# A two-layer hybrid decoder trunk on one core: another planning of its order, an earlier first weight block, and another start

## The chip, the cores and the metric

The kernel runs on one core of a Trainium2 chip. The metric is the device time of one execution in microseconds: the median of 3 runs before is 1589.41 us (1588.22 to 1592.01).

## What is computed

Two layers over 512 positions of width 1024, all in float32. Cut to what matters:

```python
for i in range(2):
    h = rmsnorm(x, mix_pre_g[i]);  z = h @ w_in[i]              # 1024 -> 3206 columns, split over three mixers
    # A: chunked causal spatial gating on u, v;  B: chunkwise retention on q, k, v, g (6 heads, rotary)
    # C: forgetting attention on q, k, v, f (6 heads, softmax over s <= t)
    x = x + rmsnorm(concat(A, B, C) @ w_o[i], mix_post_g[i])
    h = rmsnorm(x, ffn_pre_g[i])
    g = causal_dwconv3(h @ w_gate[i]);  f = (gelu(g) * (h @ w_up[i])) @ w_down[i]      # 1024 -> 4096 -> 1024
    x = x + rmsnorm(f, ffn_post_g[i])
    gate = sigmoid(rmsnorm(x, ple_pre_g[i]) @ w_ple_gate[i])
    x = x + rmsnorm((p[i] @ w_ple_proj[i]) * gate, ple_post_g[i])
```

## The kernel before

The program is written as a list of operations, and a planner (class Plan) decides their order on each engine. It keeps every operation with its reads, writes and an estimated cost, plays them through a model of the engines, and gives each engine the earliest recorded operation among those that are ready; then all operations are issued in that order. An operation may take a buffer ahead of the oldest unfinished operation only within a number of operations that belongs to its stage (AHEAD: mix for the mixers, wo and wo2 for the two halves of the output projection, emb for the p projection, gu0 and gu for the gate/up blocks, dn, end, pg, pg2), and only if the buffers that the recorded order needs up to there are not more than there are. There are 24 large buffers of 8 KB a partition (18 of set X, 6 of set W; wg, wsa and wsb must lie in W, other fp32r tiles in X, float32 tiles in either), 12 work tiles (wk) and 8 PSUM banks. All instructions are issued on one line (L444), so the profile is read by tile names.

Precise products are made of three fp32r matmuls: each operand is split into a rounded high part (a cast on ACT) and the rest (a subtraction on DVE), and mm3 multiplies high by high, high by low and low by high. The function split issues these two instructions. Transposes, the small attention and retention products and the cumulative sums are float32 matmuls.

The stages of a layer:

- The mixers. Plain makes hT, the transposed operand of the normed rows: for each chunk of 128 positions and each half of the columns a multiplication by the norm vector (tile gain), four transposes into hps, a split. Its scale method makes the row factors rs (square and row sum on ACT, power on POOL). The steps run in the order written in mixers: u is the gating projection (weights uv, eight blocks of k, chunk after chunk in tm_chunk_major; its PSUM tiles are called ps), F and v the other value projections, f0 to f2, r0 to r2 and g0 to g2 the projections of heads (fps, rps, gps), a0 to a2 attention, c0 to c2 the retention cores, s the spatial gating, L a silu.
- out_proj: the concatenated result cc times w_o, first all four chunks in the first half of the columns (PSUM tiles wo, the blocks of cc in O_ORDER), then the second half chunk by chunk in the order 0, 2, 1, 3. After each chunk of the second half, done normalises and stores the row and hands it to Seven, which makes the seven operands of the FFN product (tiles hb, hh, hd) by transposes, sums and splits.
- ffn: the p projection (embed, PSUM tiles eps), then 32 gate/up blocks and the down product (dn). gate_up computes a 2 x 2 block product with seven instead of eight multiplications. For each block it loads raw weights (graw, two transfers of 512 KB), splits wg and wu, forms sums and differences in place with four additions, and splits these to wsa and wsb; then seven products of 12 matmuls go to the PSUM tiles beta and ag. From block 4 on TensorE's order is fixed by a fence; before that the planner mixes.
- ple: the gate and the last residual.

At the start the program loads the rows of x chunk by chunk (512 KB each), the identity, the norm vector (a broadcast to all partitions, 512 KB) and the uv weights in four transfers of 512 KB, all from SP except the identity, which ACT issues.

## Time and profile before

| | us |
|---|---|
| median of 3 runs | 1589.41 |
| lowest, highest | 1588.22, 1592.01 |
| the profiled execution | 1587.76 |
| its span, first to last instruction | 1585.7 |
| PE busy in the span | 1559.8 (98%) |
| DVE busy | 1233.2 (78%) |
| ACT busy | 837.2 (53%) |
| DMA, mean | 125 GB/s |

Times are microseconds from the span's start. PE is TensorE's matmul row, PEld its weight loads, DVE is VectorE, ACT ScalarE, POOL GpSimd, and SPq the transfers that SyncE issues. The ends of matmuls are modelled, so the pitch of their starts says more than their durations. The clock column is the granted clock of TensorE as a share of 2.4 GHz: 1.00 or 0.50.

### The profile page before, as it was taken

The page shows a single profiled execution, that of the slowest core. Times are in us where ns is not written, and L with a number is a line of the kernel's source. Part 1 is how long each engine was busy: PE and PEld are TensorE (multiplying, and loading weights), DVE is VectorE, ACT ScalarE, POOL GpSimd, SP SyncE. Part 2 cuts the span into 40 slices and gives each one's busy share as a digit, 9 for nine tenths or more (in the row PEclk, how much of TensorE's full clock was granted, in tenths as well). Part 3 has the DMA queues.
Part 4 walks back from the last instruction along what each step waited for, and adds up shares of the span by engine and source line. Part 5 has one row for each costly group of instructions (what it writes and reads, how often), then busy time and mean ns, then how long its engine had stood idle before and what let it go on. Part 6 is the DMA issues. An engine that isn't in the chain of part 4 may idle for free.

```text
span 1585.7 us, 25202 instructions
## 1 busy us (share of the span) xinstructions
PE 1559.8 (98%) x10034; PEld 1388.1 (88%) x10034; DVE 1233.2 (78%) x2013; ACT 837.2 (53%) x1380; POOL 91.3 (6%) x157
## 2 busy tenths in 40 slices
PE   7999998999999999999999999989999999999998
PEld 6887787999999999998888777889999999999987
DVE  6556869988878888878664658699887897898785
ACT  7324637665555555554552446477655555555453
POOL 1100020000000000002220000200000000000021
PEclk9999999999999999999999999999999999999999
DMA  8113147223323422424463023362332233234433
GB/s 316 68 55 107 61 168 265 81 80 115 125 81 103 137 80 88 153 100 180 179 250 107 28 80 116 125 252 81 108 116 97 92 123 106 83 131 134 148 141 124
DMA packets 63421, 197.47 MB, mean 125 GB/s; under 512 B 7348, under 2 KB 15164, under 8 KB 63304
## 3 DMA queue, kind: packets, MB, share of 16 engines
q1 hardware_dynamic: 63160, 195.81, 35.1%
q8 instruction: 78, 1.28, 0.3%
q14 instruction: 39, 0.32, 0.1%
q10 hardware_dynamic: 144, 0.07, 0.0%
HBM read 178.52 MB, written 17.33 MB: 124 GB/s over the span
## 4 chain that ended last, share of the span: by engine, by line
PE 95%; DVE 2%; DMA 1%; ACT 1%; POOL 0%; issue 0%; SPq 0%; POOLq 0%; DVEq 0%; ACTq 0%
PE beta L444 22%; PE dn L444 22%; PE ag L444 16%; PE ps L444 15%; PE rps L444 4%; PE fps L444 4%; PE gps L444 2%; PE wo L444 2%; PE sps L444 1%; PE hps L444 1%; PE tps L444 1%; PE ops L444 1%; PE rops L444 1%; DMA graw<-in_w_gu_dram 1%; PE ips L444 0%
## 5 line engine op out<-in xcount | busy, mean ns | idle before, releaser
L444 PE MATMUL dn<-thl,act 128*128 128x512 f32 x1536 | 371.4, 391 | 0.0
L444 PEld LDWEIGHTS dn<-thl,act 128*128 128x128 f32 x1536 | 279.9, 188 | 51.9
L444 PE MATMUL ps<-thl,hT 128*128 128x512 f32 (+3 forms) x984 | 207.1, 368 | 0.1
L444 PEld LDWEIGHTS ps<-thl,hT 128*128 128x128 f32 x984 | 177.0, 189 | 23.3 <-DVE thl L444 1.2
L444 DVE TENSOR_TENSOR graw<-graw 128x512 f32<-128x512 f32 x256 | 169.2, 684 | 1.0
L444 DVE TENSOR_TENSOR thl<-traw,thl 128x1024 fp32r<-128x1024 f32 (+2 forms) x120 | 140.4, 1184 | 13.6 <-ACT thl L444 13.6
L444 ACT CAST thl<-traw 128x1024 fp32r<-128x1024 f32 (+2 forms) x120 | 120.1, 1018 | 9.0 <-DMA traw<-in_w_pg_dram 4.6
L444 PE MATMUL beta<-hh,wsa 128*128 128x256 f32 x768 | 101.4, 281 | 7.8 <-ACT gs L444 7.5
L444 PEld LDWEIGHTS beta<-hh,wsa 128*128 128x128 f32 x768 | 94.7, 192 | 8.7 <-ACT gs L444 7.9
L444 PEld LDWEIGHTS beta<-hb,wg 128*128 128x128 f32 x768 | 97.7, 189 | 4.9
L444 PEld LDWEIGHTS beta<-hh,wu 128*128 128x128 f32 x768 | 98.2, 189 | 4.2
L444 PE MATMUL beta<-hh,wu 128*128 128x256 f32 x768 | 100.4, 280 | 0.0
L444 PE MATMUL beta<-hb,wg 128*128 128x256 f32 x768 | 99.9, 278 | 0.0
L444 PE MATMUL ag<-hb,wg 128*128 128x256 f32 x768 | 98.6, 276 | 0.0
L444 PE MATMUL ag<-hd,wsa 128*128 128x256 f32 x768 | 98.5, 278 | 0.0
L444 PE MATMUL beta<-hh,wsb 128*128 128x256 f32 x768 | 98.4, 276 | 0.0
L444 DVE SCALAR_TENSOR_TENSOR cv<-gs,cw,cv 128x511 f32<-128x511 f32 (+1 forms) x128 | 95.1, 743 | 3.6 <-ACT cv L444 3.5
L444 PE MATMUL ag<-hb,wsb 128*128 128x256 f32 x768 | 97.9, 276 | 0.0
L444 ACT ACTIVATE cv<-gs,cw 128x512 f32<-128x512 f32 x64 | 52.2, 816 | 82.4 <-DVE gs L444 82.4
L444 ACT COPY gs<-beta 128x256 f32<-128x256 f32 x128 | 47.2, 371 | 88.4 <-PE beta L444 86.6
L444 DVE TENSOR_TENSOR wsb<-graw,wsb 128x1024 fp32r<-128x1024 f32 x64 | 78.0, 1219 | 19.8 <-ACT wsb L444 15.0
L444 PEld LDWEIGHTS ag<-hd,wsa 128*128 128x128 f32 x768 | 93.1, 190 | 0.0
(193 smaller groups left out, 2655.7 us busy)
## 6 DMA issues: line engine op xcount, KB each, us to landing
graw<-in_w_gu_dram SPq DMA_DIRECT2D x128, 512.0 KB, 6.2
traw<-in_w_dn_dram SPq DMA_DIRECT2D x64, 512.0 KB, 5.0
x<-x SPq DMA_DIRECT2D x40, 512.0 KB, 5.0
fraw<-in_w_fm_dram SPq DMA_DIRECT2D x30, 512.0 KB, 8.8
traw<-in_w_wo_dram SPq DMA_DIRECT2D x16, 512.0 KB, 4.2
traw<-in_w_pg_dram SPq DMA_DIRECT2D x16, 512.0 KB, 8.6
x<-in_x_dram SPq DMA_DIRECT2D x8, 512.0 KB
traw<-in_w_uv_dram SPq DMA_DIRECT2D x8, 512.0 KB, 8.1
```

Of the source, the lines that this page charges most:

```text
L444: made = o[1](*[self.map(v) for v in o[2]], **{k: self.map(v) for k, v in o[3].items()})
```

## The change

- The planner: limits ahead are other numbers, most of them larger; a buffer that all its users have left is no longer counted as occupied until its place in the recorded order (the two lines with -= 1). The costs of matmul kinds and of changes between kinds are other numbers, and its clock model stays at the upper level once reached. An operation can be put behind another (behind).
- The mixers' steps come in another order, and two blocks of cc change places in O_ORDER.
- The preparation of a gate/up block's weights is a function of its own. That of block 0 is recorded inside out_proj, after the first chunk of the second half (EARLY).
- The start: x's first chunk and the norm vector are loaded in halves of 256 KB, the former from SP, the latter from ACT; the first layer's uv weights come in eight transfers of 256 KB and are split one block of k at a time; the row factors are put behind the last of these splits in the plan. Ten bf16 matmuls of 512 columns on a tile of zeros are recorded ahead of everything.

```diff
--- before.py
+++ after.py
...
@@ -59,12 +59,12 @@
-    AHEAD = {"mix": 460, "wo": 230, "wo2": 230, "emb": 185, "gu0": 720, "gu": 460, "dn": 245, "end": 770, "pg": 450, "pg2": 120}
+    AHEAD = {"mix": 595, "wo": 404, "wo2": 214, "emb": 291, "gu0": 1206, "gu": 523, "dn": 1028, "end": 1710, "pg": 555, "pg2": 142}
     LOAD = 1290
...
     TABLES = (AF.Exp, AF.Gelu_apprx_tanh, AF.Silu, AF.Sigmoid, AF.Sin)
-    SWITCH = {"F": 110, "T": 9}
+    SWITCH = {"F": 40, "H": 310, "T": 9}
     HOP = {"PE": 197, "DVE": 128, "ACT": 131, "POOL": 80, "SP": 0}
...
@@ -189,6 +190,8 @@
                 t[2].append((i, write, r))
+        if self.behind is not None:
+            deps.add(self.behind)
         if engine == "PE":
...
@@ -220,10 +223,11 @@
             dt, rows = kw["lhsT"].dtype, kw["lhsT"].shape[0] / P
-            if dt == F32R:
+            if dt in (F32R, BF16):
                 return 0.4427 * n, 0, n * rows, n
-            half = 0.5 if kw["lhsT"].shape[0] == 64 or kw["lhsT"].shape[-1] == 64 else 1
-            return half * max(222, n * 4 / 2.4 + 4), 0, 2 * n * rows, "F"
+            if kw["lhsT"].shape[0] == 64 or kw["lhsT"].shape[-1] == 64:
+                return 0.5 * (n * 4 / 2.4 + 4), 0, 2 * n * rows, "H"
+            return max(222, n * 4 / 2.4 + 4), 0, 2 * n * rows, "F"
         if engine == "ACT":
...
@@ -356,8 +360,10 @@
                     heapq.heappush(slots[tag], now)
+                    live[tag][front:last[t] + 1] -= 1
                     if t in self.kind:
                         c, k = self.place[t]
+                        inside[c][front:last[t] + 1] -= 1
                         heapq.heappush(unused[c], (now, k))
...
@@ -402,13 +408,14 @@
                         if ops[i][6][3] != kind:
-                            busy += self.SWITCH.get(kind, 0) + (95 if ops[i][6][3] == "F" else 25 if ops[i][6][3] == 512 else 0)
+                            busy += self.SWITCH.get(kind, 0) + {"H": 95, 512: 25}.get(ops[i][6][3], 0)
                             kind = ops[i][6][3]
                     if e == "PE":
-                        if columns.get(now // self.TICK - 1, 0) < self.WARM:
+                        if not warm:
                             busy *= 2
-                        tick = (now + busy) // self.TICK
-                        columns[tick] = columns.get(tick, 0) + ops[i][6][2]
+                            tick = (now + busy) // self.TICK
+                            columns[tick] = columns.get(tick, 0) + ops[i][6][2]
+                            warm = columns.get(now // self.TICK - 1, 0) >= self.WARM
                     if self.table.get(i) not in (None, table):
...
@@ -483,7 +490,11 @@
 FM_COLS = [c + p * P for p in range(3) for c in (C_RQ, C_RK)] + [C_RG + p * P for p in range(3)] + [c + p * P for p in range(3) for c in (C_FQ, C_FK)]
-O_ORDER = (0, 1, 5, 6, 7, 2, 3, 4)
+STEPS = "u g1 F g0 f0 s v f1 a0 g2 L a1 f2 r0 r1 a2 c0 r2 c2 c1"
+O_CHUNKS = (0, 2, 1, 3)
+EARLY = {0: 0}
+O_ORDER = (0, 1, 5, 6, 7, 2, 4, 3)
+IDLE = 10
 SEVEN = ("hb11", "hb21", "hh6", "hd", "hh7", "hb22", "hh4")
...
@@ -652,11 +663,11 @@
-        def __call__(self, c, x):
+        def __call__(self, c, x, halves=range(2)):
             if self.t is None:
...
                 self.rs = small("rs", NCH)
-            for kh in range(2):
+            for kh in halves:
                 cs = slice(kh * 512, kh * 512 + 512)
...
@@ -1062,7 +1073,7 @@
         fq, rq = {}, {}
-        for step in "u F s g1 f0 g0 v a0 f1 a1 g2 r0 f2 L c0 r1 a2 r2 c1 c2".split():
+        for step in STEPS.split():
             h = int(step[1]) if len(step) > 1 else 0
...
@@ -1092,7 +1105,26 @@
-    def out_proj(l, cc, x, new, g, nxt):
+    def gate_up_weights(l, b):
+
+        stage, plan.stage = plan.stage, "gu0" if b < 4 else "gu"
+        raw = b8("graw", (2048,))
+        load(raw, a["w_gu"][l, b].rearrange("p s n -> p (s n)"))
+        u2, u1, g1, g2 = (raw[:, i * 512:i * 512 + 512] for i in range(4))
+        wg = b8("wg", (2, 1024), F32R)
+        split(wg[:, 0, :], wg[:, 1, :], raw[:, 1024:2048])
+        wu = [wk("wu", dt=F32R) for _ in range(2)]
+        split(wu[0], wu[1], u2)
+        for t, by in ((g1, u1), (u1, u2), (u2, g1), (g2, u2)):
+            V.tensor_tensor(out=t, in0=t, in1=by, op=ALU.add)
+        sa = b8("wsa", (2, 1024), F32R)
+        split(sa[:, 0, :], sa[:, 1, :], raw[:, 0:1024])
+        sb = b8("wsb", (2, 1024), F32R)
+        split(sb[:, 0, :], sb[:, 1, :], raw[:, 1024:2048])
+        plan.stage = stage
+        return wg, wu, sa, sb
+
+    def out_proj(l, cc, ready, x, new, g, nxt):
...
@@ -1114,10 +1146,15 @@
             nxt(c, x[c])
-        tm_chunk_major(cc, u, 512, done, O_ORDER, (0, 2, 1, 3))
+            if len(seen) in EARLY:
+                ready[EARLY[len(seen)]] = gate_up_weights(l, EARLY[len(seen)])
+            seen.append(c)
+
+        seen = []
+        tm_chunk_major(cc, u, 512, done, O_ORDER, O_CHUNKS)
         return emb
-    def ffn(l, hs, emb, x, new, g, nxt):
+    def ffn(l, hs, emb, ready, x, new, g, nxt):
         h = hs.t
...
@@ -1135,20 +1172,7 @@
         def gate_up(b, between):
-            raw = b8("graw", (2048,))
-            load(raw, a["w_gu"][l, b].rearrange("p s n -> p (s n)"))
-            u2, u1, g1, g2 = (raw[:, i * 512:i * 512 + 512] for i in range(4))
-            wg = b8("wg", (2, 1024), F32R)
-            split(wg[:, 0, :], wg[:, 1, :], raw[:, 1024:2048])
-            wu = [wk("wu", dt=F32R) for _ in range(2)]
-            split(wu[0], wu[1], u2)
-            for t, by in ((g1, u1), (u1, u2), (u2, g1), (g2, u2)):
-                V.tensor_tensor(out=t, in0=t, in1=by, op=ALU.add)
-            sa = b8("wsa", (2, 1024), F32R)
-            split(sa[:, 0, :], sa[:, 1, :], raw[:, 0:1024])
-            sb = b8("wsb", (2, 1024), F32R)
-            split(sb[:, 0, :], sb[:, 1, :], raw[:, 1024:2048])
-
+            wg, wu, sa, sb = gate_up_weights(l, b) if b not in ready else ready[b]
             beta, ag = bank("beta"), bank("ag")
...
@@ -1337,29 +1361,62 @@
+    idle = wk("idle", dt=BF16)
+    G.memset(idle, 0.0)
+    ps = bank("idle")
+    for i in range(IDLE):
+        T.matmul(ps, lhsT=idle[:, 0:P], rhs=idle, start=True, stop=True)
+
     x = Rows(x0)
-    x.load(0)
+    x.t[0] = b8("x", (2, D))
+    g = Gains(None, ("mix_pre_g", 0))
+    g.t = b8("gain", (2, D))
+    raws = [b8("traw", (4, 512)) for _ in range(2)]
+
+    def half(i):
+        cs = slice(i * 512, i * 512 + 512)
+        SY.dma_start(out=x[0][:, cs], in_=x0[:, 0, cs])
+        A.dma_start(out=g.t[:, 1, cs], in_=a["mix_pre_g"][0:1, cs].to_broadcast([P, 512]))
+
+    half(0)
     ident = const("ident", A)
-    g = Gains(None, ("mix_pre_g", 0))
+    SY.dma_start(out=raws[0][:, 0, :], in_=a["w_uv"][0][:, 0, :])
+    half(1)
+    for k in range(1, KB):
+        SY.dma_start(out=raws[k // 4][:, k % 4, :], in_=a["w_uv"][0][:, k, :])
     hT = Plain(g)
-    hT(0, x[0])
-    uv = tm_units(a["w_uv"][0], 512)
+    parts = []
+    for k in range(KB):
+        if k % 4 == 0:
+            hT(0, x[0], (k // 4,))
+        if k % 2 == 0:
+            parts.append(b8("thl", (2, 2, 512), F32R))
+        split(parts[-1][:, 0, k % 2, :], parts[-1][:, 1, k % 2, :], raws[k // 4][:, k % 4, :])
+
+    last = len(plan.ops) - 1
+
+    def uv(i, k, c0=0, c1=512):
+        return parts[k // 2][:, i, k % 2, c0:c1]
+
     for c in range(1, NCH):
...
         hT(c, x[c])
+    plan.behind = last
     for c in range(NCH):
         hT.scale(c, x[c])
+    plan.behind = None
     kdec = const("kdec")
...
     for l in range(DEPTH):
-        cc = mixers(l, hT, uv)
+        ready = {}
+        cc = mixers(l, hT, uv, ready)
         g = Gains(("mix_post_g", l), ("ffn_pre_g", l))
         hs = Seven(g)
-        emb = out_proj(l, cc, Rows(src), xd[3 * l], g, hs)
+        emb = out_proj(l, cc, ready, Rows(src), xd[3 * l], g, hs)
         g = Gains(("ffn_post_g", l), ("ple_pre_g", l))
         hT = Plain(g)
-        ffn(l, hs, emb, Rows(xd[3 * l]), xd[3 * l + 1], g, hT)
+        ffn(l, hs, emb, ready, Rows(xd[3 * l]), xd[3 * l + 1], g, hT)
         last = l + 1 == DEPTH
```

## Rows read from the trace of the kernel before

**Rows 1.** The head of the page: the span, and the busy time of each engine with its share and its number of instructions.

```profile
span 1585.7 us, 25202 instructions
PE 1559.8 (98%) x10034; PEld 1388.1 (88%) x10034; DVE 1233.2 (78%) x2013; ACT 837.2 (53%) x1380; POOL 91.3 (6%) x157
```

**Rows 2.** Who waited for whom, on PE, over the whole span: us in total, times, longest.

```profile
PE hps L444 <- DVE h L444: 7.9, 1, 7.9
PE beta L444 <- ACT gs L444: 7.5, 2, 3.8
PE hps L444 <- ACT wg L444: 1.8, 2, 0.9
PE cps L444 <- DVE ro L444: 1.2, 2, 0.7
```

**Rows 3.** The chain of waits in order of time: start, length, what. The first two are the first real matmuls and transposes of the second chunk, the third the rest of the gating projection.

```profile
9.95 6.26 PE ps L444 x17
16.21 0.44 PE hps L444 x4
...
21.45 15.47 PE ps L444 x68
```

**Rows 4.** The timeline of the first 30 us, of SPq, ACT, DVE, PE and POOL: start, length, engine, operation, count; in brackets the engine's idle time before it and what ended it.

```profile
0.79 0.39 SPq L444 DMA_DIRECT2D x<-in_x_dram  x1
...
1.22 1.28 ACT L444 ACT_TABLE_LOAD   x1 [1.22 <-PEq L1382]
1.24 0.42 SPq L444 DMA_DIRECT2D gain<-in_mix_pre_g_dram  x1
1.71 1.97 SPq L444 DMA_DIRECT2D traw<-in_w_uv_dram  x4
...
4.61 1.06 ACT L444 ACTIVATE junk<-x 128x1024 bf16<-128x1024 f32 x1 [2.11 <-DMA x<-in_x_dram]
...
7.14 1.29 DVE L444 TENSOR_TENSOR h<-x,gain 128x512 f32<-128x512 f32 x2 [7.14 <-DMA gain<-in_mix_pre_g_dram]
...
8.37 1.04 ACT L444 CAST thl<-traw 128x1024 fp32r<-128x1024 f32 x1 [2.60 <-DMA traw<-in_w_uv_dram]
...
9.44 1.22 DVE L444 TENSOR_TENSOR thl<-traw,thl 128x1024 fp32r<-128x1024 f32 x1 [1.01 <-ACT thl L444]
...
11.79 3.49 DVE L444 TENSOR_TENSOR thl<-traw,thl 128x1024 fp32r<-128x1024 f32 x3
...
15.19 3.10 DVE L444 TENSOR_TENSOR h<-x,gain 128x512 f32<-128x512 f32 x5
...
26.01 0.99 POOL L444 TENSOR_SCALAR_AFFINE_SELECT sguw<-sguw 128x512 f32<-128x512 f32 x1 [5.58 <-DMA sguw<-in_sgu_w_dram]
```

**Rows 5.** Windows of the start: stretch, its length, busy time (and instructions) of PE, PEld, DVE, ACT and POOL, granted clock, share of the DMA engines, GB/s.

```profile
0.00:7.89 7.89, 0.00 (x0) 0.00 (x1) 0.75 (x2) 2.43 (x3) 1.14 (x8) 1.00 0.74 238
7.89:14.00 6.11, 6.02 (x17) 4.30 (x18) 5.10 (x6) 5.53 (x7) 0.00 (x0) 1.00 1.02 418
```

**Rows 6.** Windows, with the same columns, around the entry of the gate/up loop in layer 0 (205 to 300) and layer 1 (from 1045).

```profile
205.00:245.00 40.00, 39.49 (x210) 32.44 (x209) 26.75 (x43) 18.21 (x40) 8.75 (x19) 1.00 0.36 142
245.00:258.70 13.70, 12.76 (x64) 10.15 (x64) 12.15 (x19) 11.47 (x22) 2.06 (x4) 1.00 0.57 172
...
261.70:265.70 4.00, 0.23 (x3) 0.03 (x1) 4.00 (x8) 2.29 (x5) 0.00 (x0) 1.00 1.02 395
...
266.40:269.80 3.40, 3.10 (x16) 2.81 (x15) 3.40 (x5) 1.64 (x3) 0.00 (x0) 0.50 1.04 420
270.00:300.00 30.00, 30.00 (x267) 30.00 (x266) 28.98 (x44) 19.80 (x33) 0.00 (x0) 1.00 0.41 151
...
1049.30:1054.90 5.60, 5.60 (x26) 5.58 (x27) 5.60 (x8) 2.71 (x4) 0.00 (x0) 0.50 1.04 417
```

**Rows 7.** The timeline at that entry, of PE and DVE: the end of the operands (hh), the end of wsa, and PE's waits in layer 0 and, last row, in layer 1.

```profile
261.78 0.68 DVE L444 TENSOR_TENSOR hh<-s,hh 128x512 fp32r<-128x512 f32 x1
...
265.68 0.51 PE L444 MATMUL beta<-hh,wsa 128*128 128x256 f32 x2 [3.77 <-ACT gs L444]
...
266.00 1.22 DVE L444 TENSOR_TENSOR wsa<-graw,wsa 128x1024 fp32r<-128x1024 f32 x1
...
1049.28 0.80 PE L444 MATMUL beta<-hh,wsa 128*128 128x256 f32 x2 [3.75 <-ACT gs L444]
```

**Rows 8.** Instructions on the tile graw between 180 and 300 us: shortest, median and longest in ns, first and last start in us.

```profile
L444 DVE TENSOR_TENSOR graw<-graw x20: 676/681/684, 260.0 to 298.9; 128x512 f32<-128x512 f32 x20
L444 SPq DMA_DIRECT2D graw<-in_w_gu_dram x16: 328/432/1090, 204.4 to 297.5; - x16
L444 ACT CAST wu<-graw x5: 618/620/632, 224.2 to 274.7; 128x512 fp32r<-128x512 f32 x5
L444 ACT CAST wg<-graw x5: 1050/1053/1061, 252.6 to 275.2; 128x1024 fp32r<-128x1024 f32 x5
L444 DVE TENSOR_TENSOR wg<-graw,wg x5: 1211/1216/1219, 254.1 to 285.7; 128x1024 fp32r<-128x1024 f32 x5
```

**Rows 9.** The timeline at the end of layer 0's mixers: PE's wait for the second last retention core, then the last core from the end of rops (where wo goes on) to its place in cc.

```profile
205.89 0.66 PE L444 MATMUL cps<-k_ident,ro 128*128 128x128 f32 x4 [0.51 <-DVE ro L444]
...
212.23 4.83 PE L444 MATMUL wo<-thl,cc 128*128 128x512 f32 x20
...
219.92 0.69 DVE L444 TENSOR_TENSOR cc<-og,cc 128x512 fp32r<-128x512 f32 x1 [0.69 <-ACT cc L444]
```

More of the change, by code (lines that the diff above doesn't have):

```diff
@@ L78, in __init__ @@
         self.group, self.follows = None, {}
+        self.behind = None
         self.stage, self.stages = "mix", []
@@ L283, in issue @@
         order = []
-        then, kind = None, "T"
+        then, kind, warm = None, "T", False
         parked = {tag: [] for tag in (*slots, *(f"b8 {k}" for k in (*self.SETS, None)))}
@@ L816, in body, with mixers @@
     cums = [[dram(f"cums{l}_{h}", (1, S)) for h in range(6)] for l in range(DEPTH)]
-    def mixers(l, hT, uv):
+    def mixers(l, hT, uv, ready):
         rs = hT.rs
@@ L1082, in mixers @@
                 A.activation(sg, sg, AF.Silu)
+            elif step[0] == "p":
+                ready[h] = gate_up_weights(l, h)
             elif step[0] == "f":
```

## The prediction

> **What bounds the kernel now.** Read the page's head first: TensorE is busy 98% of the span [rows 1]. It is nearly the whole path, so only two things can shorten the run: moments when it stands, and moments at the lower of its clock levels. Second, the list of who waited for whom on PE [rows 2] says where it stands: 7.9 us at the start, for the first product h; 7.5 us in two waits for gs; some 3 us in all the rest. Third, the chain of waits [rows 3] gives the pitch of a matmul of 512 columns: 68 in 15.47 us, 0.228 us each. Against that the first 17 take 6.26 us, 0.368 each, although the clock column reads 1.00 there [rows 5]: the column has no record yet that early, the pitch has. Behind the 7.89 us of standing still the first of them run at 1.2 GHz and later ones at 2.4. Fourth, the windows around the entry of the gate/up loop [rows 6] show the same effect with the clock on record: after a 4 us hole the granted clock is 0.50 for 3.4 us in layer 0 and 5.6 us in layer 1. So the losses that can be had are 7.9 + about 3 us at the start, and per layer one hole with its slow stretch. The long stretch of FFN and the other projections runs at its pitch.
>
> **The start.** Now SP issues x (512 KB) at 0.79, the norm vector at 1.24, four weight parts from 1.71; x is used at 4.61, the vector lands at 7.14, the first weights at 8.37 [rows 4]. The first real matmul starts at 9.95. After the change the first product needs 256 KB of x and 256 KB of the vector. x took 3.8 us from issue to use; the vector landed 2.5 us after it, the next 512 KB 1.2 us after that. Half of each is x about 0.6 sooner and a vector share of 1.25 instead of 2.5: h starts at about 4.6 instead of 7.14. From h to the first real matmul it is 2.81 us now; four transposes of the eight (0.44 [rows 3]), a cast and a subtraction stay, so 2.3 to 2.8: the first real matmul at about 7.0 (some three us earlier). The second queue by itself saves little: SP issues one transfer in 0.39 to 0.49 us, while between 7.89 and 14 us the DMA engines' share is 1.02 at 418 GB/s [rows 4, 5]. The Trainium skill ("DMA: Bandwidth & Descriptors", section "Issuing engines are not separate DMA queues") says that transfers issued from two engines run on the same 16 DMA engines and save only the issuing time. By that rule the second queue alone is worth some 0.45 us, and the forecast below would not change if the queue were left out; that the start gives only this much is a rival.
>
> The weights decide from there. Until the last uv weight the bytes are the same 3.1 MB (x 0.5, vector 0.5, identity 0.06, weights 2.0). 7.89 us at 238 GB/s are 1.88 MB, the remaining 1.25 MB at 418 GB/s take 3.0 us [rows 5]: about 10.9, some 11.3 with the landing. A cast and a subtraction of half the present size (1.04 and 1.22 us [rows 4]) end at 12.4, where the last weight subtraction now ends at 15.28 (11.79 + 3.49) because DVE began late. The second chunk's rows land at about 12.5; its multiplication, now at 15.19, starts near 12.6, and its first matmul near 14.4 (0.69 + 0.44 + a cast of 0.6). Chunk 0's 24 matmuls fit before it (24 x 0.228 = 5.5 us from 7.0, paced by the weights to 12.8). Left then are 72 matmuls (16.4), 20 transposes (2.2) and some 0.6 of changes between the two: 33.6, where this group now ends at 36.92 (21.45 + 15.47). **Gain 3.0**, ends 1.0 (small packets and interleaving put the weights 2 us later) and 5.0 (no gap between chunks 0 and 1). What is late next is the second chunk's rows, not the vector.
>
> The ten zero matmuls have no row: no bf16 matmul ran. By the 512 column pitch they are 2.3 us at the upper and 4.6 us at the lower level. They wait for a memset on POOL, at most the 0.99 us of the nearest 512 element row [rows 4]; they end between 3.6 and 6.5. That is before or about when the first transposes are ready, and up to 1 us of overlap is hidden by the weight-paced stretch until 12.8. I take zero cost, and full clock from about 7 on. If the zeros do not raise the clock, the first stretch goes at the pitch that it has now: 17 x (0.368 - 0.228) = 2.4 us of the gain are lost again. On ACT three issues (1.2 us) stand before the table load of 1.28 us [rows 4], both over before the first cast at some 5.5. The row sums of the chunks are put behind the last weight subtraction, 4 x 1.06 us of ACT [rows 4]; the gelu that waits for them only holds a PSUM bank of eight.
>
> **The gate/up entry.** In the hole at 261.7 PE had used wg of block 0 and needs wsa, which is complete at 267.22 [rows 7]. The operands that it also needs were there earlier (hh's last subtraction 262.46). wsa is late because block 0's 512 KB parts were requested from 204.4 on, but the first wg is cast at 252.6 [rows 8]: preparation sits in the queue behind the last chunk's norm, with DVE busy 12.15 of 13.70 us and 4.00 of 4.00 [rows 6]. The change records block 0's preparation after the first chunk of out_proj, so ahead of three chunks in priority. It costs DVE 3 x 1.22 + 5 x 0.68 = 7.1 us (wu's subtraction has the form of the four additions) and ACT 3 x 1.05 + 0.62 = 3.8 us per layer [rows 8]. From 205 to 245 DVE is busy 26.75 of 40 us and ACT 18.21 [rows 6]: 13 and 22 us free, so it fits beside TensorE's work there. SP's two graw issues and 1 MB (2.5 us at 418 GB/s) move into a stretch with a DMA share of 0.36. Then at 258.7 block 0 needs only the operands: its seven products are 84 matmuls of 256 columns, half of 0.228 each, 9.5 us of work, in which DVE prepares block 1.
>
> Per layer this takes away: layer 0, the hole of 3.77 [rows 7] and half of 3.40 us at 0.50 [rows 6] = 5.5; layer 1, 3.75 [rows 7] and half of 5.60 [rows 6] = 6.6. Together 12.1. Two things eat of it. Memory: the three W tiles that block 0 holds are missing for chunk 2's seven operands, so two of these wait until cc and the wo weights are free at 245; 2 x (0.62 + 0.68) us of ACT and DVE go into the tail, 1.3 us on DVE. And DVE stays nearly full in the blocks that follow (28.98 of 30 us from 270 to 300 [rows 6]), so a backlog can show up later as short waits. **Gain 11.5**, ends 4 (both holes go by a third only) and 13 (waits of the transposes there go too).
>
> **The rest.** The planner's costs, clock model and limits, and the credit for buffers returned early, add no instruction; they change the order. So do the new order of the mixers' steps and the change of blocks 3 and 4. PE's waits outside the two places above are 1.8 + 1.2 us [rows 2]; removing them is at best 3, with the changes between float32 and fp32r matmuls perhaps 4. Against that, each retention core ends in a serial chain of 8.4 us (rops' end 212.23, cc complete 220.61 [rows 9]), covered now by out_proj's matmuls except for 0.5 us. I take **1.0 gain**, ends -4 and +4, nearest to the row of 1.2.
>
> **Sum.** 3.0 + 11.5 + 1.0 = 15.5. The profiled execution took 1587.76 us, its span 1585.7 us: 1572.3, span 1570.2. The median of the runs lies 1.65 us above the profiled one, so 1573.9 by the median; I say 1574.
>
> **Rivals.** (a) The start gives only the issue time, because both queues share the same transfers and chunk 1 arrives when it does now: -0.5 instead of -3: 1576.5. For it speaks the DMA share of 1.02; against it, DVE's late 15.19, which is no transfer. 0.13. (b) The entry's hole moves: DVE's backlog or the delayed operands of chunk 2 make PE wait at block 1 instead, and with 4 us it loses the clock again; gain 5 instead of 11.5: 1580.5. For it: DVE's 28.98 of 30; against it: the 13 us free before 245. 0.17. (c) The order does not do what it says: block 0's W tiles come free no earlier than at 250, and only the start is won: 1586. 0.05. (d) Slower: at the end of the mixers core 2 follows its own projection at once and its block is now consumed seventh; six blocks (72 matmuls, 16.4 us) instead of seven cover it. If both late cores' chains of 8.4 us lie open in both layers, that is 34 us against 14.5 won: 1608. It decides from 3.6 us open per core on; now 0.5 is open [rows 9]. 0.08. (e) Better: all of the entry, 4.5 at the start and the small waits, 1568. 0.10. The forecast has 0.47.
>
> **How the numbers follow.** The range takes in (a), (b) and (e) and the bounds of the start and the entry; it leaves out (c), (d) and the extremes: 1567 to 1582. A measurement of this kernel can tell about 0.2%, 3 us. Slower by more than that: (d) and a little of the unknown order, 0.09; within: (c) and part of the low ends, 0.06; faster: 0.85.
>
> **What would show it.** The first ps matmul at about 7 and at a pitch of 0.228, uv finished near 33.6; no wait of beta for gs in the list, granted clock 1.00 through both entries, wg cast before 245. Wrong would be: a wait of PE over 2 us anywhere between the mixers and the third gate/up block, a row of 0.50 in the clock, or the list of PE's waits with cps or hps above 3 us.

## The result, and the profile after

| us | before | after |
|---|---|---|
| median of 4 runs | 1588.99 | 1578.30 |
| lowest, highest | 1588.22, 1592.01 | 1577.73, 1579.93 |
| the profiled execution | 1587.76 | 1579.93 |
| its span | 1585.7 | 1578.2 |

The ratio is 0.9931, with a 95% interval of 0.9914 to 0.9948: faster by 10.7 us, where 15.5 were forecast. The time lies inside the range of 1567 to 1582, 4.3 us above the value. (The kernel before has one run more here than the table ahead of the prediction.) The profiled execution of after is the longest of its four, so the two traces show 7.6 us of the 10.7.

The page's head of after, beside [rows 1]: TensorE is busy 99% of the span.

```profile
span 1578.2 us, 25255 instructions
PE 1562.7 (99%) x10044; PEld 1390.1 (88%) x10044; DVE 1229.4 (78%) x2017; ACT 838.0 (53%) x1382; POOL 94.5 (6%) x158
```

Who waited for whom on PE in after, beside [rows 2] (engine, tile, releaser: us in all, times, the longest):

```profile
PE hps L451 <- DVE h L451: 2.1, 5, 0.7
PE hps L451 <- DMA k_ident<-in_c_ident_dram: 1.8, 1, 1.8
PE idle L451 <- POOL idle L451: 1.4, 1, 1.4
PE tps L451 <- DVE pe L451: 0.7, 2, 0.4
...
PE beta L451 <- ACT gs L451: 0.6, 2, 0.4
```

The 7.9 us before the first h are gone from the list, and the two waits of beta for gs have shrunk from 7.5 to 0.6 us. TensorE is busy 2.9 us longer than before all the same, with a span that is 7.6 us shorter: part of what was standing still has become busy time that is slow or new (the ten zero matmuls alone take 3.73 us).

**The entry of the gate/up loop.** The windows of after around it in layer 0, and one of layer 1 (stretch, length, then busy time and count of PE, PEld, DVE, ACT and POOL, the granted clock, the DMA share, GB/s), beside [rows 6]:

```profile
205.00:245.00 40.00, 39.51 (x189) 32.08 (x188) 29.22 (x41) 18.29 (x39) 8.62 (x17) 1.00 0.26 97
245.00:259.40 14.40, 14.07 (x71) 11.34 (x70) 13.60 (x21) 13.12 (x26) 3.42 (x6) 1.00 1.00 333
259.40:270.00 10.60, 10.60 (x92) 10.56 (x91) 10.60 (x18) 9.52 (x18) 0.00 (x0) 1.00 0.95 362
...
1039.00:1055.00 16.00, 16.00 (x143) 16.00 (x141) 16.00 (x26) 13.95 (x23) 0.00 (x0) 1.00 1.00 377
```

The clock stays at 1.00 (2.4 GHz) through both entries, and TensorE is busy all the time once the blocks have begun. The raw weights' tile in after, 180 to 300 us, beside [rows 8], and TensorE's timeline there, beside [rows 7]:

```profile
L451 ACT CAST wg<-graw x7: 1039/1077/1113, 222.8 to 289.8; 128x1024 fp32r<-128x1024 f32 x7
L451 ACT CAST wsa<-graw x5: 1037/1049/1057, 230.3 to 295.7; 128x1024 fp32r<-128x1024 f32 x5
```

```profile
259.47 1.58 PE L451 MATMUL beta<-hb,wg 128*128 128x256 f32 x12
...
260.88 1.58 PE L451 MATMUL ag<-hb,wg 128*128 128x256 f32 x12
...
262.65 1.58 PE L451 MATMUL beta<-hh,wsa 128*128 128x256 f32 x12
```

wg is cast from 222.8 on instead of 252.6, wsa from 230.3 instead of 264.3, and the products of block 0 follow each other with no stand between them. DVE has 2.5 us more to do between 205 and 245 than before, and TensorE is as busy there (39.51 us, before 39.49).

**The start.** The same views of after, beside [rows 5] and [rows 4]:

```profile
0.00:7.89 7.89, 4.36 (x14) 1.63 (x14) 1.27 (x2) 2.18 (x3) 0.80 (x7) 0.99 0.72 210
7.89:14.00 6.11, 5.09 (x13) 3.73 (x14) 4.71 (x9) 4.26 (x9) 0.00 (x0) 0.50 1.00 334
```

```profile
1.45 3.73 PE L451 MATMUL idle<-idle 128*128 128x512 bf16 x10 [1.45 <-POOL idle L451]
...
2.16 7.55 SPq L451 DMA_DIRECT2D traw<-in_w_uv_dram  x7
...
5.84 0.69 DVE L451 TENSOR_TENSOR h<-x,gain 128x512 f32<-128x512 f32 x1 [5.84 <-DMA gain<-in_mix_pre_g_dram]
...
6.95 0.63 PE L451 MATMUL hps<-k_ident,h 128*128 128x128 f32 x4 [1.77 <-DMA k_ident<-in_c_ident_dram]
...
8.25 1.22 PE L451 MATMUL ps<-thl,hT 128*128 128x512 f32 x2 [0.67 <-ACT hT L451]
...
9.39 0.69 DVE L451 TENSOR_TENSOR h<-x,gain 128x512 f32<-128x512 f32 x1 [1.38 <-DMA gain<-in_mix_pre_g_dram]
9.75 1.38 SPq L451 DMA_DIRECT2D x<-in_x_dram  x3
...
10.13 1.11 PE L451 MATMUL hps<-k_ident,h 128*128 128x128 f32 x4 [0.67 <-DVE h L451]
...
10.90 6.96 PE L451 MATMUL ps<-thl,hT 128*128 128x512 f32 x22
...
16.33 2.55 DVE L451 TENSOR_TENSOR h<-x,gain 128x512 f32<-128x512 f32 x4 [0.73 <-DMA x<-in_x_dram]
...
17.70 1.47 PE L451 MATMUL hps<-k_ident,h 128*128 128x128 f32 x12
```

The first product of h starts at 5.84 instead of 7.14, the first real matmul at 8.25 instead of 9.95. Yet the last uv matmul starts at 36.66 from the span's beginning, before at 36.54: the lead is lost on the way.

SP needs 7.55 us for seven weight issues, so that the second chunk's rows are asked for at 9.75 (before at 3.72). The list of SP's waits says what it stood for:

```profile
SPq L451 <- DMA gain<-in_mix_pre_g_dram: 4.2, 2, 2.6
```

Before the first of these two waits eight transfers had been issued, five from SP and three from ACT, and SP went on only when a half of the vector had landed, twice. The rate between 7.89 and 14 falls from 418 to 334 GB/s. The vector's second half is there at 9.39, later than the whole of it before (7.14). The second chunk's multiplication starts at 16.33, before it was 15.19.

But TensorE does not wait for that multiplication. After the wait of 0.67 us for the vector's second half, which ends at 10.13, it has no wait until uv is done: the 22 matmuls that are left of chunk 0 fill the time up to 17.70, and the second chunk's transposes follow at once. What makes this stretch long is the clock. TensorE stood from 5.18 to 6.95 and then had little to do until 10.90, and its granted clock is 0.50 (1.2 GHz) from 7.89 to 14; up to 14.56 the matmuls start 0.43 us apart, after that 0.23. Nine of them at the slow pitch cost some 1.8 us (an estimate: 9 x 0.2). With a full clock the second chunk's rows would have been the limit soon after, at about 17.0 (16.33 and one multiplication of 0.69), so the two limits lie within 0.7 us of each other.

**Where the time went**, from the starts of single matmuls in both traces, both layers added (start: up to the last uv matmul; mixers: up to the last matmul ps <- cc of out_proj; entry: up to the 151st matmul dn, so with the p projection and the first blocks; ffn: up to the last dn; rest: gates, second layer's uv, end). Kernels of the experiments stand below:

```
               start   mixers   entry     ffn    rest     span
before         36.54   415.58  317.96  690.42  125.24   1585.7
after          36.66   418.07  306.21  691.88  125.35   1578.2
old_start      36.58   418.12  305.61  692.50  125.11   1577.9
only_start     36.32   415.67  319.03  690.44  125.40   1586.9
no_early       36.16   416.18  316.94  692.47  125.73   1587.5
early_only     37.53   417.55  323.13  690.46  125.26   1593.9
early_credit   36.51   422.72  309.93  691.00  125.98   1586.1
no_credit      36.28   431.61  333.81  691.08  135.15   1627.9
old_ahead      36.15   435.29  319.12  690.85  124.89   1606.3
old_steps      35.63   423.63  308.16  697.25  124.93   1589.6
eight          38.62   418.13  305.87  692.32  125.23   1580.2
pairs          36.27   418.02  307.24  691.83  125.37   1578.7
one_queue      37.91   418.11  305.41  692.05  125.29   1578.8
zeros24        38.96   418.09  305.22  691.97  125.41   1579.6
```

After against before: the entries give 11.75, the start costs 0.1, the mixers with out_proj cost 2.5, ffn 1.5, the rest 0.1: 7.6 net. Five kernels differ from after in the start alone (old_start and the last four rows): their entries are 305.2 to 307.2, their mixers within 0.1, so the entry's figure is good to about 1 us, the mixers' to 0.1.

### The profile page after: what moved, and what is told of

Read it like the earlier page. It is cut to its first block, busy times and chain, and to the rows that moved or that the text cites. A ratio compares the mean times of both kernels' runs of the same rounds, so it can differ in the third digit from the quotient of the medians.

```text
span 1578.2 us, 25255 instructions
## 1 busy us (share of the span) xinstructions
PE 1562.7 (99%) x10044; PEld 1390.1 (88%) x10044; DVE 1229.4 (78%) x2017; ACT 838.0 (53%) x1382; POOL 94.5 (6%) x158
## 5 line engine op out<-in xcount | busy, mean ns | idle before, releaser
L451 DVE TENSOR_TENSOR thl<-traw,thl 128x1024 fp32r<-128x1024 f32 (+3 forms) x124 | 141.7, 1158 | 24.1 <-ACT thl L451 24.1
L451 ACT CAST thl<-traw 128x1024 fp32r<-128x1024 f32 (+3 forms) x124 | 121.4, 995 | 40.5 <-DVE wsb L451 19.3
L451 PE MATMUL beta<-hh,wsa 128*128 128x256 f32 x768 | 97.9, 277 | 0.0
L451 ACT ACTIVATE cv<-cv 128x512 f32<-128x512 f32 x64 | 40.5, 632 | 107.7 <-DVE cv L451 107.7
L451 PEld LDWEIGHTS beta<-hh,wsb 128*128 128x128 f32 x768 | 92.3, 188 | 1.1 <-ACT gs L451 1.0
L451 PEld LDWEIGHTS ag<-hb,wg 128*128 128x128 f32 x768 | 92.8, 188 | 0.3
```

The lines of the kernel that those rows point to most:

```text
L451: made = o[1](*[self.map(v) for v in o[2]], **{k: self.map(v) for k, v in o[3].items()})
```

## The experiments

The theory behind the first of them: the early block of weights makes the gain, and the start gains almost nothing. Its rival was the prediction's account, in which the start gives 3 us and the planner's parts 1. That the planner's parts are conditions of the early block came out of the runs; the expectations had it for the credit alone. Each time below is a median with its ratio to the kernel before, run on the same chip.

**old_start**: the changed kernel with the start of before.

```diff
-    half(0)
-    SY.dma_start(out=raws[0][:, 0, :], in_=a["w_uv"][0][:, 0, :])
-    half(1)
...
+    x.load(0)
+    hT(0, x[0])
+    uv = tm_units(a["w_uv"][0], 512)
```

> The changed kernel with the start of the kernel before (512 KB transfers from SP, no zeros, no halves), all else as changed. Theory (the new start gained nothing: uv ended at 36.89 us against 36.77): within 1 us of the changed kernel's 1578.3, uv's last matmul at 36.5 to 37.2. Rival (the start did give its 3 us and the mixers lost them again): 1581.

1579.67 us, 0.9947 (0.9934 to 0.9959); the interval overlaps that of the change, and the time lies midway between what theory and rival expected. The trace gains 7.8 us of span without the new start, where the change gained 7.6 with it.

**only_start**: the kernel before with the new start alone (halves, eight parts, ten zeros, the row factors behind the splits).

> The kernel before with the new start alone (halves, two queues, eight weight parts, ten zero matmuls; costs and limits of the planner as before). Theory: 1588 to 1590, as before, uv's end within 0.5 us of 36.8, a clock of 0.50 somewhere between 7 and 15 us. Rival (the start is worth 3 us): 1586, uv's end near 33.8.

1586.89, 0.9991 (0.9982 to 1.0). The start is worth 1.7 us by the medians here (1588.62 - 1586.89), and 1.7 by old_start too (the change gains 10.69 over its kernel before, old_start 8.95 over its own). By the traces it is less: six kernels with the new start unaltered (after, only_start, no_early, no_credit, old_ahead, old_steps) end it at 35.63 to 36.66, median 36.22; four with the old one (before, old_start, early_only, early_credit) at 36.51 to 37.53, median 36.56. So 0.3 to 1.7, against 3.0 forecast. The interval of only_start allows 0 to 2.9 us. Neither expectation of only_start held: the time was under the theory's, the end of uv far from the rival's.

**no_early**: the changed kernel, block 0 prepared in its old place.

```diff
-EARLY = {0: 0}
+EARLY = {}
```

> The changed kernel with EARLY empty: block 0's weights are recorded in ffn again. Theory (the early block carries the whole gain at the entry, 5.4 + 7.0 us by the profile, and costs some 0.8 us a layer of transposes that wait for DVE in out_proj): 1588 to 1590, holes of about 4 us at both entries with a clock of 0.50 behind them. Rival (the credit for early returned buffers and the larger limits bring the weights early anyway): 1578 to 1581, no holes.

1590.02, 1.0014 (1.0005 to 1.0022): nothing is left of the gain. The entries return to 316.94. The time is at the upper edge of what was expected, its cause is another: there is no hole of 4 us now, the clock stays at 1.00 through both entries, and the loss is spread over waits of up to 1.3 us, in the list of PE's waits:

```profile
PE ag L451 <- DVE gs L451: 3.9, 4, 1.3
PE beta L451 <- DVE wsa L451: 3.6, 4, 1.3
```

It also shows the price of the early block: mixers with out_proj take 416.18 without it and 418.07 with it, 0.95 a layer.

**old_steps**: the changed kernel with the old order of the mixers' steps and of the blocks of cc.

```diff
-STEPS = "u g1 F g0 f0 s v f1 a0 g2 L a1 f2 r0 r1 a2 c0 r2 c2 c1"
+STEPS = "u F s g1 f0 g0 v a0 f1 a1 g2 r0 f2 L c0 r1 a2 r2 c1 c2"
...
-O_ORDER = (0, 1, 5, 6, 7, 2, 4, 3)
+O_ORDER = (0, 1, 5, 6, 7, 2, 3, 4)
```

> The changed kernel with the mixers' old order of steps and the old O_ORDER. Theory (the new order lost some 1.2 us a layer between uv's end and the last chunk of out_proj, as the profile's milestones say): 1576. Rival (that loss comes from block 0's preparation in out_proj and the order is worth something): 1579 to 1582.

1591.69, 1.0019 (1.001 to 1.0028). Both expectations missed: with the other edits in place the order is worth some 13 us. 5.6 of it lies in the mixers and out_proj and 5.4 in ffn. Its waits, as the first places of PE's list have them:

```profile
PE ag L451 <- DVE gs L451: 3.9, 11, 0.4
PE cps L451 <- DVE ro L451: 2.8, 4, 1.0
```

cps <- ro is at the end of the retention cores. ag <- gs comes back along ffn, far from the steps that were changed; how the order of the mixers reaches there (the place of a tile, the phase of the fixed order) was not followed up.

**early_only**: the kernel before with block 0's preparation moved, and nothing else.

```diff
+            if len(seen) in EARLY:
+                ready[EARLY[len(seen)]] = gate_up_weights(l, EARLY[len(seen)])
```

> The kernel before with block 0's weights recorded in out_proj, nothing else changed: old limits, costs, order of steps, start, no credit for returned buffers. Theory (the place in the record is what removes the holes): no waits of 3.8 us at the entries, clock 1.00 there, 1588.6 - 11 = 1578. Rival (without the credit the W tiles are not given to the block before the last chunk, so it comes late as now): 1587 to 1590.

1595.47, 1.0038 (1.0025 to 1.0052): slower. wg is cast from 228.4 on, as wanted, and the hole has moved. PE's first wait, its timeline at the entry, ACT's sum of squares for the last chunk, the start of its copies of the p projection, and two windows:

```profile
PE hps L444 <- DVE h L444: 18.4, 6, 7.9
```

```profile
250.52 1.64 PE L444 MATMUL eps<-ehl,pT 128*128 128x512 f32 x6
256.94 1.97 PE L444 MATMUL hps<-k_ident,h 128*128 128x128 f32 x8 [4.78 <-DVE h L444]
...
253.84 1.06 ACT L444 ACTIVATE junk<-x 128x1024 bf16<-128x1024 f32 x1
...
255.92 1.56 ACT L444 COPY e<-eps 128x512 f32<-128x512 f32 x3
```

```profile
251.00:255.00 4.00, 1.16 (x5) 0.59 (x4) 4.00 (x7) 3.10 (x7) 0.00 (x0) 1.00 0.54 154
255.00:262.00 7.00, 5.06 (x16) 4.37 (x17) 6.19 (x12) 5.41 (x11) 0.79 (x2) 0.51 0.96 301
```

DVE works 4.00 of 4.00 us on other operands. The row h of the last chunk waits for its row factor, whose sum of squares ACT begins only at 253.84, behind such operands too; DVE multiplies h at 256.14. The matmuls eps that could fill the time do not run (their results are copied out from 255.92, in after from 247.76: no room, it seems), and when TensorE comes back its clock is 0.50. That is the mechanism of rival (b), at the last chunk's transposes instead of block 1, and with a loss in the entries (5.2) where (b) still had a gain of 5.

**early_credit**: that kernel and the two lines that count returned buffers as free.

```diff
+                    live[tag][front:last[t] + 1] -= 1
...
+                        inside[c][front:last[t] + 1] -= 1
```

> The kernel before with block 0's weights recorded in out_proj and the two lines that credit returned buffers; limits, costs, order of steps and start as before. Theory (early_only's new hole of 4.9 us at eps and hps came from buffers that the planner held back, so that the copies of the p projection started at 255.9 instead of 248.5; the credit gives them cc's and the weights' buffers): the hole of 4.8 us goes, clock 1.00 at both entries, 1588 - 9 = 1579. Rival (the larger limits are what is needed): 1590 to 1596, the hole stays.

1588.33, 0.9996 (0.9987 to 1.0004), which neither expected. The hole is gone, so it did come from buffers that were held back. The entries win 8.0, with the clock at 1.00; the mixers and out_proj lose 7.1 of them. That the planner, free to take buffers earlier, then takes the wrong things first there is only argued.

**no_credit**: the changed kernel without those two lines.

> The changed kernel without the two lines that stop counting returned buffers. Theory (the credit is needed, because the recorded order wants 26 large tiles at the second chunk and there are 24): block 0's first wg is cast after 245 us and the holes are back: 1587 to 1591. Rival (the larger limits are enough): 1577 to 1580.

1631.38, 1.0266 (1.0252 to 1.028): the worst of all. The first places of PE's waits:

```profile
PE hps L449 <- DVE h L449: 10.0, 4, 4.4
PE beta L449 <- ACT gs L449: 9.2, 7, 3.8
```

wg of block 0 is cast at 224.5 here too, so the early record does what it says. The losses lie in what stands behind it: the entries (+27.6 against after), the mixers and out_proj (+13.5), and the gate of layer 0 with the second layer's uv (81.7 instead of 71.7). Neither expectation had this. The two lines are the only edit, so the losses come from buffers that stay counted as taken; which buffers, and which steps they hold back, was not followed up.

**old_ahead**: the changed kernel with the old limits.

```diff
-    AHEAD = {"mix": 595, "wo": 404, "wo2": 214, "emb": 291, "gu0": 1206, "gu": 523, "dn": 1028, "end": 1710, "pg": 555, "pg2": 142}
+    AHEAD = {"mix": 460, "wo": 230, "wo2": 230, "emb": 185, "gu0": 720, "gu": 460, "dn": 245, "end": 770, "pg": 450, "pg2": 120}
```

> The changed kernel with the limits ahead (AHEAD) of the kernel before. Theory (credit and early record carry the gain, the limits only shift single waits): 1577 to 1582, entries within 2 us of the changed kernel's. Rival (the larger limits are needed as well): the holes of about 4 us are back, 1588 or more.

1607.82, 1.0117 (1.0104 to 1.013). The rival's time, but most of it is not in the holes that the rival named: the mixers lose 17.2 against after, the entries 12.9, with single waits of 1.7 us at most and a clock of 0.50 for 6.8 us in each layer. TensorE's timeline at the end of layer 0's mixers in it, the same place in after, and the window of it around this:

```profile
193.92 1.16 PE L451 MATMUL ips<-rm 64*128 64x128 f32 x16 [4.11 <-DVE rm L451]
...
197.82 1.23 PE L451 MATMUL kvps<-mix,kt 128*64 128x64 f32 x12 [1.05 <-DVE kt L451]
198.97 4.34 PE L451 MATMUL wo<-thl,cc 128*128 128x512 f32 x12
```

```profile
189.70 0.62 PE L451 MATMUL wo<-thl,cc 128*128 128x512 f32 x2
190.25 1.66 PE L451 MATMUL ips<-rm 64*128 64x128 f32 x16
...
193.17 0.71 PE L451 MATMUL wo<-thl,cc 128*128 128x512 f32 x2
```

```profile
190.00:216.00 26.00, 21.03 (x129) 18.10 (x130) 24.05 (x41) 11.16 (x15) 8.10 (x6) 0.87 0.39 135
```

In after the first matmuls of out_proj (wo) run from 189.70 on, between the steps of a retention core. With the old limits the first of them comes at 198.97, so the core's steps lie open, TensorE is busy 21.03 of 26 us (25.79 in after), and its clock is 0.87 in the mean. That is the place of rival (d) and, by chance, its time of 1608.

**eight, pairs, one_queue, zeros24**: four other starts of the changed kernel, to see what holds the start.

```diff
eight:      uv weights in 3 transfers
+    SY.dma_start(out=raws[0][:, 1:4, :], in_=a["w_uv"][0][:, 1:4, :])
+    SY.dma_start(out=raws[1], in_=a["w_uv"][0][:, 4:8, :])
pairs:      uv weights in four transfers of two blocks of k
+    for k in range(2, KB, 2):
+        SY.dma_start(out=raws[k // 4][:, k % 4:k % 4 + 2, :], in_=a["w_uv"][0][:, k:k + 2, :])
one_queue:  pairs, and the vector's halves from SP ahead of the weights
+        SY.dma_start(out=g.t[:, 1, cs], in_=a["mix_pre_g"][0:1, cs].to_broadcast([P, 512]))
zeros24:
+IDLE = 24
```

> The changed kernel with the first uv weights in three transfers (one, three and four blocks of k) instead of eight, so that everything the first chunk needs is eight transfers. Theory (a ninth transfer is issued only when the first has landed; with halves and eighths only half the bytes are under way, and SP asks for the second chunk's rows at 9.75 us instead of 3.72): SP asks for them before 7 us, their multiplication starts at 14.6 or sooner instead of 16.33, uv's last matmul starts at 35.2 or sooner instead of 36.66, the time is 1.5 us under the changed kernel. Rival (the transfers are as fast as the engines allow, and 2 KB packets and the broadcast decide): multiplication at 16 or later, uv's end at 36.5.

1582.25, 0.9959 (0.9946 to 0.9971). The window from 8 to 12 us, and when SP asks for the second chunk's rows and DVE multiplies them:

```profile
8.00:12.00 4.00, 2.93 (x8) 1.54 (x7) 1.42 (x3) 1.09 (x3) 0.00 (x0) 1.00 1.00 416
```

```profile
6.07 1.47 SPq L451 DMA_DIRECT2D x<-in_x_dram  x3
...
16.93 3.10 DVE L451 TENSOR_TENSOR h<-x,gain 128x512 f32<-128x512 f32 x5
```

The rows are asked for 3.7 us sooner and the rate is back at 416 GB/s, as expected; yet the multiplication is later, and the last uv matmul starts at 38.62, later than theory and rival had it. The theory that the issue's wait alone holds the start falls. Two things came on top: the weights now come in lumps, and the casts with them (TensorE waits 0.77 us for one at 12.65), and the matmuls start 0.43 us apart until 17.23, in after until 14.56.

> The changed kernel with the first uv weights in four transfers of two blocks of k (512 KB, as before the change) instead of eight of one; x and the norm vector still in halves, zeros as changed. Theory (small transfers, of which only eight may be under way, hold the rate at 334 GB/s from 7.89 to 14 us where it was 418; the lumps of 0.75 and 1 MB in the run called eight brought the first weights too late): 400 GB/s or more in that window, the second chunk's multiplication at 15.0 or sooner instead of 16.33, uv's last matmul at 35.5 or sooner, 1 us or more under the changed kernel. Rival (DVE's own work in the start decides, however the weights are cut): 36.3 to 37.

1580.56, 0.9949 (0.9936 to 0.9961). 407 GB/s between 7.89 and 14, the second chunk at 16.21, the last uv matmul at 36.27. The theory falls: the rate is won, and does not decide. The rival's time came true, but no wait shows DVE as the reason.

> The run called pairs with the norm vector's halves issued by SP again, both before the weights (x half, vector half, x half, vector half, then four weight parts); ACT issues the identity alone. Theory (on two queues the vector's halves and the identity share the engines packet by packet with x and the weights, so the identity lands at 6.95 and the vector's second half at 9.39 instead of 7.14, and DVE, which has 8 us of work in a row for the first chunk, stands until then): no wait of PE for the identity, the second half's multiplication at 8.0 or sooner, the second chunk's at 15.0 or sooner instead of 16.33, uv's last matmul at 35.5 or sooner. Rival (the latency of the first chunk's steps on DVE and ACT, or the clock at 0.50, decides however the parts arrive): second chunk at 15.8 or later, uv's last matmul at 36.0 to 36.8.

1580.46, 0.9942 (0.9929 to 0.9956). The identity is no longer waited for, but DVE's timeline has

```profile
6.09 0.69 DVE L451 TENSOR_TENSOR h<-x,gain 128x512 f32<-128x512 f32 x1 [6.09 <-DMA gain<-in_mix_pre_g_dram]
8.98 0.69 DVE L451 TENSOR_TENSOR h<-x,gain 128x512 f32<-128x512 f32 x1 [2.20 <-DMA gain<-in_mix_pre_g_dram]
...
16.24 3.09 DVE L451 TENSOR_TENSOR h<-x,gain 128x512 f32<-128x512 f32 x5
```

and the last uv matmul starts at 37.91, later than theory and rival had it. The order of the queues is not it either: the vector, as a broadcast in halves, is late from either queue, and the clock is back at 1.00 only at 16.14.

> The changed kernel with 24 zero matmuls instead of ten, so that TensorE runs until the first product is there. Theory (the rows of the second chunk hold the gating projection, not the clock): the granted clock stays 1.00 after the zeros, but uv's last matmul stays at 36.3 to 37.0 and the time within 1 us of the changed kernel. Rival (the clock that fell to 0.50 from 7.7 to 14.6 us ate the start's gain): uv's end at 34.5, 2 us less.

1582.7, 0.9962 (0.9949 to 0.9974). Two windows and TensorE's timeline:

```profile
7.40:14.10 6.70, 4.56 (x24) 2.66 (x23) 5.47 (x9) 4.52 (x10) 0.00 (x0) 1.00 1.03 371
14.20:17.50 3.30, 3.30 (x9) 2.52 (x9) 3.30 (x6) 2.59 (x5) 1.61 (x2) 0.50 1.03 394
```

```profile
12.60 4.89 PE L451 MATMUL ps<-thl,hT 128*128 128x512 f32 x12 [2.03 <-ACT hT L451]
```

The longer run of zeros does keep the clock at 1.00 from 7.40 to 14.10, where the change had 0.50, but the transposes stand behind the zeros in TensorE's queue, the first real matmul comes at 12.60, 4.35 us later than in after, and the clock falls behind that, up to 17.57. Last uv matmul: 38.96. Both expectations missed, and the run does not say what a held clock is worth, because the zeros delayed the real work and the clock fell all the same.

In none of these four does the second chunk's multiplication come before the 15.19 of the kernel before. In two kernels with the change's own start it does (no_early 15.06, old_ahead 15.00), and uv's last matmul is still at 36.16 and 36.15. In none of the traces does TensorE wait more than 0.1 us for that multiplication. What the late ends have in common is the clock. The first transposes, the time from which the matmuls of 512 columns start 0.23 us apart and not 0.43, and the last uv matmul:

```
              transposes   full pitch   last uv
old_steps        7.53        13.12       35.63
old_ahead        6.88        14.12       36.15
no_early         6.86        14.44       36.16
pairs            7.77        12.09       36.27
no_credit        7.06        14.16       36.28
only_start       7.12        13.81       36.32
early_credit     7.88        13.42       36.51
before           7.89        13.82       36.54
old_start        7.81        13.42       36.58
after            6.95        14.56       36.66
early_only       7.91        16.15       37.53
one_queue        6.84        16.14       37.91
eight            7.08        17.23       38.62
zeros24          9.53        17.57       38.96
```

The four traces in which the clock came back late are the four in which uv ends late; early_only has the same start as before. Among the other ten, within 1 us, the clock alone does not give the order. No run changes the clock alone, so its share stays an estimate.

None of the twelve kernels is faster than the change.

## Why the prediction was right, and which steps were off

The entry, three quarters of the forecast gain, carried it. The start and the rest both missed to the same side, the rest by the traces as far as its lower bound, and the time still lies 3.7 us inside the range.

**The entry: right, in mechanism and in size.** 11.5 was forecast; the traces show 5.35 in layer 0 and 6.40 in layer 1, 11.75. All the marks named for it came true: no hole for gs, clock 1.00, wg cast before 245 (222.8). no_early gives the gain back alone. The size is right; the reason given for it, free time on DVE, is not enough, as early_only shows with a loss of 5.2 at the same place: that the credit, the limits and the order would be there to let the block work was not part of the step.

**The price of it: the work fits on DVE, but not at nothing.** "13 and 22 us free, so it fits" was right for DVE and ACT. Still out_proj is 0.95 a layer longer with the early block, which the step had at zero. Which of its waits pays this was not settled.

**The start: the step that failed.** 3.0 was forecast with ends of 1 and 5; the runs give 0.3 to 1.7. The first product came at 5.84 (forecast 4.6), the first real matmul at 8.25 (7.0), the second chunk's multiplication at 16.33 (12.6), its transposes at 17.70. From there to the last uv matmul it is 19.0 us, about what the step had for this work (16.4 + 2.2 + 0.6). So the loss lies before. Two assumptions failed. One let all bytes run at 418 GB/s and gave half a transfer half the time of a whole one: the vector's second half came at 9.39, SP's issues waited for the vector's halves to land, the rate was 334 GB/s. The other is "full clock from about 7 on": the clock was 0.50, chunk 0's 24 matmuls lasted from 8.25 to 17.70 instead of the 5.5 us of work at 0.228 each, and TensorE did not wait for the second chunk's rows, which the step names as what is late next. The step itself has the price of a slow clock, 2.4 us, as the case that it did not take. How much of the missing time the clock makes and how much the late landings is not separated by a run, because either limit is reached within 0.7 us of the other.

Rival (a) was nearest here, in size: it had 0.5. The Trainium skill's rule ("DMA: Bandwidth & Descriptors", section "Issuing engines are not separate DMA queues") is that a second issuing engine saves issuing time alone. This case's traces agree: with parts of 512 KB the rate is 407 GB/s with two queues (pairs) and 413 with one (one_queue).

**The zeros: cost nothing, gain nothing that shows.** Ten took 3.73 us and ended at 5.18, in the forecast stretch. "Full clock from about 7 on" was wrong: TensorE stood until 6.95 for the identity, which ACT now issues behind the vector's half, and the clock is 0.50 until 14. A row of 0.50 was one of the prediction's own signs of being wrong; it shows in the start, not at the entries.

**The rest: the wrong sign.** +1.0 was forecast, with ends of -4 and +4; by the traces it is -4.0 (2.5 in mixers and out_proj, 1.9 of them the price of the early block; 1.5 in ffn). With the medians, and the entry as the traces have it, the rest is -1.4 to -2.8 (10.7 - 11.75, less 0.3 to 1.7 for the start). The 1.5 in ffn is in no_early (2.1) and old_start (2.1) too, so neither the early block nor the start makes it. It is nearly gone without the limits (690.85), without the credit (691.08), and with the credit on the old limits (early_credit, 691.00), while the seven traces with both have 691.8 to 692.5: most of it comes with limits and credit together. Why is left open.

**The planner's parts: mis-seen.** The prediction says that they "add no instruction; they change the order", and put them at 1 us. In the change they come with the early block and let it work. Alone the early block makes the kernel 7 us slower through rival (b)'s hole; with the credit it is even; without the credit the full change is 43 us slower than before, without the limits 19, without the order 3. So (b) is what happens with the early block alone, and the time of (d) comes when the limits are missing; the reasons given against them (13 us of DVE free, six blocks of cover) were not what decides. One rival stands: limits and order may have been fitted to the full set, so that undoing any one of them breaks the fit. The runs show that the parts need each other; what limits or order bring by themselves on the kernel before was not run, and the planner's costs and clock model were not undone at all.

## What to carry to other kernels

Work moved ahead of a loop's entry must have room twice over: free time on its engine, and buffers that the order counts as free; look at both, and at what stands behind it in the queue, before the gain is counted. A transfer cut in half does not land in half the time: here the second half of a broadcast landed later than the whole had, the issuing queue waited for it, and twice as many weight transfers of half the size went with a rate that was an eighth to a fifth lower. Before a late operand is blamed for a late end, see whether the engine waits for it at all: here it was still busy, at half its clock. When edits of a plan come together, undo each by itself: here each of the four parts that were undone alone cost more than the whole had gained; only the start cost less.

## What the runs showed of the hardware

- Eight weight transfers of 256 KB beside the vector's halves: 332 to 368 GB/s from 7.89 to 14 us in seven traces (after 334, at a DMA share of 1.00). With parts of 512 KB 407 (pairs) and 413 (one_queue), with three parts 419 (eight), with the start of before 416 to 418, at shares of 1.01 to 1.03.
- The vector's broadcast of 512 KB was there at 7.14; cut in two, with weight transfers issued between, its second half was there at 8.36 to 9.59 from ACT's queue in the eight traces where DVE waited for it, and at 8.98 from SP's.
- Matmuls on zeros count as work for the clock. With 24 of them their starts go from 0.43 to 0.22 us apart at 7.37, and the granted clock is 1.00 from 7.40 to 14.10, until after TensorE had stood for 2.03 us. With ten it rose for a while in five of nine traces (in after from 4.37 on) and not at all in four (only_start, no_credit, old_ahead, eight), and in all nine matmuls of chunk 0 then still started 0.43 us apart.
- The 4.78 us that TensorE stood in early_only left the clock at 0.51 in the window from 255 to 262; waits of up to 1.3 us at the entries of no_early left it at 1.00.
